# A bank of scores instead of a projection bank for the sample rows' products of every natural block

## The chip, the cores and the metric

The kernel runs on one core of a Trainium2 chip, in one launch. The metric is the device time of the program in microseconds (us), the median of several runs.

## The reference

One inference step of a decoder layer, in f32. There are 1024 prompt rows and 8 sample rows (one new token each for 8 sequences), a model width of 1024 and one combined input projection:

```python
def _project(x, norm_g, w_in, qn_g, kn_g):
    h = _rms(x, norm_g)
    proj = jnp.einsum('bld,dn->bln', h, w_in)
    aq, ak, av, az, bu, bv, bz, cq, cf, ci, cz = jnp.split(proj, cuts, axis=-1)
...
        o_a = _dilated_prompt(aq, ak, av)                        # 12 heads of 64
        o_b, _ = _sgu(bu, bv, sgu_ln_g[l], sgu_ln_b[l], sgu_w[l], sgu_b[l])
        o_c, S_p = _hgrn2(cq, cf, ci, lb_all[l], hgrn_norm_g[l], S0)   # 6 heads of 128
        xp = _merge(xp, o_a, az, o_b, bz, o_c, cz, w_out[l])
```

The same is done for the sample rows, with attention over a cache (`_dilated_step`) and from a given recurrent state. `_merge` multiplies each branch by its gate, projects with `w_out` and adds `x`.

## The kernel before, in words

The stages stand in the program in this order: RMSNorm of the prompt and transposes to `h` (nine tiles `xt0` to `xt8`, each transposed in two `tr0` tiles; `xt8` is the sample rows, kept in f32 as `hs`), then attention, HGRN, SGU, output projection. Attention takes pairs of heads `p` = 0 to 5: block `qk{p}` is projected (four groups `pqk{p}_{g}`), the two heads `p_0` and `p_1` follow (scores for the maximum `s2_...`, transposed scores `st_...`, sums `pv{p}_{h}_{qc}`), and `normalise` (`pb{p}_0`) ends the pair. Blocks `v0` to `v2` (`pv{sp}_{g}`) and `az0` to `az2` serve two pairs each. HGRN has six heads (`c_head`, line 663, with `pn{h}_{half}` its last matmul of a half) fed by blocks `cqf{h}` (`pc...`), `ci0` to `ci2` (`pi...`) and `cz0` to `cz2`; a decode for the sample rows (`pmx`, `pda`, `pdt`) stands between the heads. SGU begins with the blocks `bv0`, `bv1` (`pbv...`), then `bz0` (`pbz0...`), `bu0` and so on.

A *block* is 256 columns of `w_in`, loaded by `load_w` (lines 190 to 208) as four pairs of 128 rows. SyncE (SP) issues the load of each pair into a tile `wr_...` of f32 ("raw"; 6 buffers, so one and a half blocks), ScalarE (ACT) rounds it into `wh_...`, GpSimd (POOL) makes the rest `wl_...` (4 buffers each). A projection is three matmuls for each 128 rows of depth, `h` and `w` each split into a high and a low part. The raw tile is held until its last reader is through: the rounding, the rest, and in the blocks `qk`, `v`, `ci`, `bv` ("natural" blocks: rows on the partitions) also the products of the 8 sample rows, `pss_...`, which take the raw f32 weights: eight matmuls, 16 records in the profile. `add_groups` (line 267) then adds their four groups, with one copy on ACT and three additions on VectorE (DVE), and frees the bank.

PSUM has eight banks: two for projections (`p_proj`), four for scores and all else of that kind (`p_st` and `p_big` share the same four, also the HGRN tiles `pk`, `lv`, `ls`, `pn`), one for transposes and decode (`p_tr`), one for sums (`p_pv`). Before, `pss_...` took a bank of `p_proj`, with the exception of `v0`, whose products and groups take banks of scores.

The order of the instructions on each engine is not the order of the code. The program is handed to a scheduler before the run, which places each instruction by its priority (where it stands in the code) and by when its inputs and a buffer are expected to be free, and hands out the buffers; the order on each engine is then fixed. So a tile that asks for a bank of another kind can move a great part of the program.

Of the kernel before, what the change touches and what calls it, by code (L numbers as in the profile page):

```python
# [91 lines left out]
def hybrid_step(tc, ins, outs, parts=("A", "D", "B", "C", "O"), dbg=None):  # L92
# [9 lines left out]
    with tc.tile_pool(name="const", bufs=1) as cp, tc.tile_pool(name="sb", bufs=1) as sb, \  # L102
# [5 lines left out]
        def inp(nm, shape=(P, L), dt=F32):  # L108
            return sb.tile(list(shape), dt, tag="big", name=nm, bufs=N_BIG)
# [10 lines left out]
        def pq(nm, shape=(P, 512), dt=F32):  # L120
            return sb.tile(list(shape), dt, tag="pq", name=nm, bufs=N_PQ)

        def small(nm, n, p=P, dt=F32, bufs=2, tag=None):
            return sb.tile([p, n], dt, tag=tag or f"sm{n}", name=nm, bufs=bufs)

        def psum(tag, nm, bufs, n=512):
            return pm.tile([P, n], F32, tag=tag, name=nm, bufs=bufs)
# [7 lines left out]
        def p_st(nm):  # L135
            return psum("st", nm, 4)
# [54 lines left out]
        def load_w(cols, nm, spare=False):  # L191
            blk = []
            for i in range(KD // 2):
                if spare:
                    hi = s2(f"wh_{nm}_{i}", F32R, (P, 2, NW))
                    lo = s2(f"wl_{nm}_{i}", F32R, (P, 2, NW)) if i < 2 else ee(f"wl_{nm}_{i}", (P, 2, NW), F32R)
                else:
                    hi = sb.tile([P, 2, NW], F32R, tag="whi", name=f"wh_{nm}_{i}", bufs=N_W)
                    lo = sb.tile([P, 2, NW], F32R, tag="wlo", name=f"wl_{nm}_{i}", bufs=N_WL)
                raw = sb.tile([P, 2, NW], F32, tag="raw", name=f"wr_{nm}_{i}", bufs=N_RAW)  # L200
                o = 0
                for c, w in cols:
                    nc.sync.dma_start(raw[:, :, o:o + w], w_in[:, 2 * i:2 * i + 2, c:c + w])
                    o += w
                nc.scalar.copy(hi, raw)
                nc.gpsimd.tensor_tensor(lo, raw, hi.bitcast(F32), ALU.subtract)
                blk.append((hi, lo, raw))
            return blk
# [10 lines left out]
        for t in (0, NT, *range(1, NT)):  # L219
# [15 lines left out]
            for j in range(2):  # L235
                ps = p_st(f"tr0_{t}_{j}").rearrange("p (a b) -> p a b", a=4)
# [16 lines left out]
        def proj_nat(blk, t, out):  # L253
            for k in range(KD):
                whi, wlo = wsl(blk, k, 0, NW)
                sl = slice(t * P, (t + 1) * P)
                mm(out, h_sl(0, k, sl), whi, k == 0, False)
                mm(out, h_sl(0, k, sl), wlo, False, False)
                mm(out, h_sl(1, k, sl), whi, False, k == KD - 1)

        def rows8(ps, K, i0=0, n=None):

            n = n or len(K)
            for i, (rows, w) in enumerate(K, i0):
                g = 32 * (i % 4)
                mm(ps[g:g + NS, :NW], rows, w, i < 4, i >= n - 4)

        def add_groups(dst, ps):
            nc.scalar.copy(dst, ps[32:32 + NS, :NW])
            for g in (64, 96, 0):  # L270
                nc.vector.tensor_tensor(dst, ps[g:g + NS, :NW], dst, ALU.add)

        def proj_nat_s(blk, nm, bank=None):
            ps = (bank or p_proj)(f"pss_{nm}")
            rows8(ps, [(hs[:, k, :], blk[k // 2][2][:, k % 2, :]) for k in range(KD)])
            dst = small(f"sd_{nm}", NW, NS, tag="sdst")
            add_groups(dst, ps)
            return dst
# [20 lines left out]
        def qk_proj(p, blk=None):  # L299
            blk = blk or load_w([(OFF_Q + p * P, P), (OFF_K + p * P, P)], f"qk{p}")  # L300
            kg = small(f"kg{p}", P, bufs=1, tag="kg")
            nc.sync.dma_start(kg, ins["k_norm_g"][:, p * P:(p + 1) * P].partition_broadcast(P)[:, 0, :])
            st = proj_nat_s(blk, f"qk{p}")
            nats = [inp(f"nat{p}_{i}", (P, 4, NW)) for i in range(2)]
            for g in range(4):
# [34 lines left out]
        def s_out(n):  # L340
            return outs[n][0, :, 0].rearrange("b h e -> b (h e)")
# [3 lines left out]
        def v_proj(sp):  # L345
            blk = load_w([(OFF_V + sp * NW, NW)], f"v{sp}") if sp else blk_v

            bank = p_proj if sp else p_st
            st = proj_nat_s(blk, f"v{sp}", bank)
            V = []  # L350
            for j in range(2):
                vh = inp(f"vh{sp}_{j}", (P, NT, VW), F32R)
                vl = inp(f"vl{sp}_{j}", (P, NT, P), F32R)
                nc.gpsimd.memset(vh.rearrange("p t (h e) -> p t h e", h=2)[:, :, :, E].bitcast(F32), 1.0)
                V.append((vh, vl))
            for g in range(4):
                ps = bank(f"pv{sp}_{g}").rearrange("p (a b) -> p a b", a=2)
                for j in range(2):
                    proj_nat(blk, 2 * g + j, ps[:, j, :])
                vr = pq(f"vr{sp}_{g}", (P, 2, NW))  # L360
                nc.scalar.copy(vr, ps)
                nc.sync.dma_start(new_v[2 * g * P:(2 * g + 2) * P, sp * NW:(sp + 1) * NW]
                                  .rearrange("(a q) c -> q a c", q=P), vr)
                if g < 2:
                    nc.sync.dma_start(v_d[2 * g * P:(2 * g + 2) * P, sp * NW:(sp + 1) * NW]
                                      .rearrange("(a q) c -> q a c", q=P), vr)
                for j in range(2):
                    vh, vl = V[j]
                    t2 = slice(2 * g, 2 * g + 2)
                    hi = vh[:, t2, :].rearrange("p a (h e) -> p a h e", h=2)[:, :, :, 0:E]  # L370
                    src = vr[:, :, j * P:(j + 1) * P].rearrange("p a (h e) -> p a h e", h=2)
                    nc.scalar.copy(hi, src)
                    nc.gpsimd.tensor_tensor(vl[:, t2, :].rearrange("p a (h e) -> p a h e", h=2), src,
                                            hi.bitcast(F32), ALU.subtract)
            nc.sync.dma_start(qkv_d[2, :, sp * NW:(sp + 1) * NW], st)
            nc.sync.dma_start(s_out("o_vs")[:, sp * NW:(sp + 1) * NW], st)
            return V
# [167 lines left out]
        def attention():  # L545
            done = None
            for sp in range(3):
                n0 = qk_proj(2 * sp, blk_first if sp == 0 else None)
                if done:
                    normalise(*done)  # L550
                tiles = qk_layout(2 * sp, n0)
                V = v_proj(sp)
                Z = az_proj(sp)
                done = attn_core(2 * sp, n0, V[0], Z[0], tiles)
                n1 = qk_proj(2 * sp + 1)
                normalise(*done)
                done = attn_core(2 * sp + 1, n1, V[1], Z[1])
            normalise(*done)
# [52 lines left out]
        def c_proj_i(hp):  # L611
            blk = load_w([(OFF_CI + hp * NW, NW)], f"ci{hp}")
            st = proj_nat_s(blk, f"ci{hp}")
            nc.sync.dma_start(qkv_d[3, :, hp * NW:(hp + 1) * NW], st)
            V = [inp(f"V{hp}_{j}", (P, NT, P)) for j in range(2)]
            for g in range(4):
                ps = p_proj(f"pi{hp}_{g}").rearrange("p (a b) -> p a b", a=2)
                for j in range(2):
                    proj_nat(blk, 2 * g + j, ps[:, j, :])
                for j in range(2):  # L620
                    nc.scalar.copy(V[j][:, 2 * g:2 * g + 2, :], ps[:, :, j * P:(j + 1) * P])
            return V
# [475 lines left out]
```

## Time and profile before

| what | value |
|---|---|
| time, median of 3 runs | 1285.43 us (1284.22 to 1287.84) |
| the profiled execution's own time | 1283.54 us |
| its span, first to last instruction | 1281.8 us |
| mean granted TensorE clock | 0.977 |
| TensorE busy (matmuls, PE) | 1206.7 us, 94% |
| VectorE busy (DVE) | 914.1 us, 71% |
| ScalarE busy (ACT) | 669.8 us, 52% |
| GpSimd busy (POOL) | 290.1 us, 23% |

The profiled execution lies 1.9 us under the median, and 1.7 us lie around its span. PE and PEld are the matmuls and the weight loads of TensorE. A granted clock of 1.00 is 2.4 GHz, one of 0.50 is 1.2 GHz. In rows of the trace an "x" is a count, and what stands in square brackets is the time that the engine was idle just before, with what ended it.

### The profile page before, as it was taken

How to read it: one execution, taken by the hardware profiler on the slowest of the kernel's cores; microseconds unless marked ns; L12 is line 12 of the kernel's file. 1: busy time of each engine (PE TensorE's matmuls, PEld its weight loads, DVE VectorE, ACT ScalarE, POOL GpSimd, SP SyncE). 2: the span in 40 equal slices, each digit the busy share in tenths (PEclk: the TensorE clock that was granted, in tenths of full speed). 3: DMA queues.
4: the chain of work that ended last, by engine and by line, in shares of the span. 5: the costliest groups of instructions: out<-in, count | busy, mean ns of one | idle time of the engine just before them, and what ended most of it. 6: DMA issues, size and time to landing. Idle time of an engine off the chain costs nothing.

```text
span 1281.8 us, 27727 instructions
## 1 busy us (share of the span) xinstructions
PE 1206.7 (94%) x10610; PEld 1119.9 (87%) x10610; DVE 914.1 (71%) x2425; ACT 669.8 (52%) x1512; POOL 290.1 (23%) x272
## 2 busy tenths in 40 slices
PE   3899999999999998998999889998999999999998
PEld 2899888998899988987988878887989899899998
DVE  4845888668876786789897898989796534654643
ACT  5445554765547565575445554665443252455543
POOL 4431201312203221122012121111011254122221
PEclk9999999999899998999999889999999999999999
DMA  7241222312223141142253514424253224621110
GB/s 224 68 136 34 65 55 79 108 37 66 71 67 100 42 117 52 25 111 84 67 146 92 131 46 139 127 80 112 81 149 97 84 75 137 194 80 47 62 47 29
DMA packets 165044, 114.17 MB, mean 89 GB/s; under 512 B 13944, under 2 KB 158992, under 8 KB 164912
## 3 DMA queue, kind: packets, MB, share of 16 engines
q1 hardware_dynamic: 157520, 110.28, 29.4%
q10 hardware_dynamic: 6816, 1.54, 0.6%
q8 instruction: 83, 1.36, 0.4%
q0 software_dynamic: 576, 0.58, 0.3%
q14 instruction: 49, 0.40, 0.1%
HBM read 84.47 MB, written 22.09 MB: 83 GB/s over the span
## 4 chain that ended last, share of the span: by engine, by line
PE 72%; DVE 16%; DMA 5%; issue 3%; ACT 3%; SPq 0%; POOL 0%; ACTq 0%; POOLq 0%; DVEq 0%
PE po L100 15%; PE pqk L100 10%; PE pv L100 9%; PE paz L100 5%; PE pi L100 4%; PE pbu L100 4%; PE pbz L100 4%; PE pcz L100 4%; PE pc L100 3%; PE pbv L100 3%; PE st L100 3%; DMA dk<-in_cache_k_dram 2%; PE s L100 2%; DVE T L647 1%; DVE T L649 1%
## 5 line engine op out<-in xcount | busy, mean ns | idle before, releaser
L100 PE MATMUL pqk<-wh_qk,h 128*128 128x256 f32 x768 | 156.6, 294 | 9.1 <-DVE h L243 4.4
L100 PE MATMUL pc<-h,wh_cqf 128*128 128x344 f32 x576 | 144.6, 331 | 10.3 <-DVE cz L152 8.8
L100 PE MATMUL po<-woh,yl 128*128 128x256 f32 x512 | 144.5, 283 | 0.0
L100 PE MATMUL po<-woh,yh 128*128 128x256 f32 x512 | 144.1, 282 | 0.3 <-ACT yh L1046 0.3
L100 PE MATMUL po<-wol,yh 128*128 128x256 f32 x512 | 143.9, 281 | 0.0
L100 PEld LDWEIGHTS pqk<-wh_qk,h 128*128 128x128 f32 x768 | 127.9, 198 | 17.0 <-DVE h L243 5.0
L100 PEld LDWEIGHTS pc<-h,wh_cqf 128*128 128x128 f32 x576 | 102.1, 194 | 13.4 <-DVE cz L152 9.7
L100 PE MATMUL pqk<-wl_qk,h 128*128 128x256 f32 x384 | 112.1, 292 | 0.0
L100 PEld LDWEIGHTS po<-woh,yl 128*128 128x128 f32 x512 | 96.6, 189 | 3.0 <-issue 1.7
L100 PEld LDWEIGHTS po<-woh,yh 128*128 128x128 f32 x512 | 96.3, 188 | 2.1 <-ACT yh L1046 2.1
L100 PEld LDWEIGHTS po<-wol,yh 128*128 128x128 f32 x512 | 96.5, 189 | 0.0
L100 PE MATMUL pc<-h,wl_cqf 128*128 128x344 f32 x288 | 95.3, 333 | 0.0
L455 DVE CUSTOM_DVE_ANT_0 s<-s,masks 128x512 f32<-128x512 f32 (+2 forms) x144 | 77.6, 576 | 19.4 <-PE s L100 18.6
L100 PE MATMUL pi<-wh_ci,h 128*128 128x256 f32 x384 | 79.1, 301 | 10.5 <-DVE cmat L722 8.1
L100 PEld LDWEIGHTS pqk<-wl_qk,h 128*128 128x128 f32 x384 | 75.7, 197 | 1.4 <-issue 0.2
L100 PEld LDWEIGHTS pi<-wh_ci,h 128*128 128x128 f32 x384 | 65.1, 204 | 13.6 <-ACT dsc L962 5.4
L100 PE MATMUL pv<-wh_v,h 128*128 128x256 f32 x384 | 75.2, 287 | 1.0 <-ACT den L516 1.0
L100 PE MATMUL pcz<-h,wh_cz 128*128 128x344 f32 x288 | 71.2, 325 | 0.2 <-DVE q L152 0.2
L100 PE MATMUL paz<-h,wh_az 128*128 128x344 f32 x288 | 68.9, 323 | 0.0
L1047 DVE TENSOR_TENSOR yl<-yb,yh 128x512 fp32r<-128x512 f32 x44 | 30.3, 692 | 52.6 <-ACT yh L1046 52.6
L100 PEld LDWEIGHTS pv<-wh_v,h 128*128 128x128 f32 x384 | 61.1, 189 | 3.1 <-ACT st L493 1.1
L1046 ACT CAST yh<-yb 128x512 fp32r<-128x512 f32 x64 | 39.5, 620 | 42.7 <-PE po L100 41.9
(389 smaller groups left out, 3586.5 us busy)
## 6 DMA issues: line engine op xcount, KB each, us to landing
wro<-in_w_out_dram SPq DMA_DIRECT2D x32, 256.0 KB
wr_qk<-in_w_in_dram SPq DMA_DIRECT2D x48, 128.0 KB
wr_cqf<-in_w_in_dram SPq DMA_DIRECT2D x48, 128.0 KB
dk<-in_cache_k_dram SPq DMA_DIRECT2D x24, 192.0 KB
dv<-in_cache_v_dram SPq DMA_DIRECT2D x24, 192.0 KB
xt<-in_x_prompt_dram SPq DMA_DIRECT2D x8, 512.0 KB
xr<-in_x_prompt_dram SPq DMA_DIRECT2D x32, 128.0 KB
out_o_yp_dram<-xr SPq DMA_DIRECT2D x32, 128.0 KB
```

The lines of the kernel that those rows point to most:

```text
L100: nc.tensor.matmul(out, lhsT=lhsT, rhs=rhs, start=start, stop=stop)
L455: nc.vector.tensor_tensor_reduce(out=ps[:, :w], in0=ps[:, :w], in1=nmask[:, S - n + c:S - n + c + w], op0=ALU.add, op1=ALU.max, scale=1.0, ...
L647: nc.vector.tensor_tensor(K.rearrange("p (n w) -> p n w", w=w), g3[:, :, w - 1:w].to_broadcast([P, 4 * n, w]), h3, ALU.subtract)
L649: nc.vector.tensor_tensor(Q[:, 0:3], g4[:, 1:4], g4[:, 0:3, :, w - 1:w].to_broadcast([P, 3, n, w]), ALU.subtract)
L1046: nc.scalar.copy(yh[:, sl, :], y)
L1047: (nc.gpsimd if piece == 0 else nc.vector).tensor_tensor(yl[:, sl, :], y, yh[:, sl, :].bitcast(F32), ALU.subtract)
```

## The change

`proj_nat_s` takes a bank of scores for every block, and its argument `bank` goes. In `v_proj` the groups `pv{sp}_{g}` keep their own kind of bank.

```diff
-        def proj_nat_s(blk, nm, bank=None):
-            ps = (bank or p_proj)(f"pss_{nm}")
+        def proj_nat_s(blk, nm):
+            ps = p_st(f"pss_{nm}")
             rows8(ps, [(hs[:, k, :], blk[k // 2][2][:, k % 2, :]) for k in range(KD)])
             dst = small(f"sd_{nm}", NW, NS, tag="sdst")
             add_groups(dst, ps)
@@
             bank = p_proj if sp else p_st
-            st = proj_nat_s(blk, f"v{sp}", bank)
+            st = proj_nat_s(blk, f"v{sp}")
```

The same instructions are issued, none more and none less: 13 tiles `pss_...` (`qk0` to `qk5`, `v1`, `v2`, `ci0` to `ci2`, `bv0`, `bv1`) change banks. But each engine's order differs in many places. Three of them:

The first is the start, on SP, which issues the loads: `xt` are the prompt's tiles, `wr_v0` and `wr_az0` weights, `ko` and `K1` results and rows of attention. Before:

```order
L222 DMA xt2_197<-in_x_prompt_dram 128x1024
L222 DMA xt3_224<-in_x_prompt_dram 128x1024
L203 DMA wr_v0_2_373<-in_w_in_dram 128x2x256
L203 DMA wr_v0_3_379<-in_w_in_dram 128x2x256
L222 DMA xt4_251<-in_x_prompt_dram 128x1024
L222 DMA xt5_278<-in_x_prompt_dram 128x1024
L203 DMA wr_az0_0_1015<-in_w_in_dram 128x2x256
L203 DMA wr_az0_1_1021<-in_w_in_dram 128x2x256
L222 DMA xt6_305<-in_x_prompt_dram 128x1024
L222 DMA xt7_332<-in_x_prompt_dram 128x1024
```

With the change:

```order
L222 DMA xt2_197<-in_x_prompt_dram 128x1024
L222 DMA xt3_224<-in_x_prompt_dram 128x1024
L222 DMA xt4_251<-in_x_prompt_dram 128x1024
L222 DMA xt5_278<-in_x_prompt_dram 128x1024
L222 DMA xt6_305<-in_x_prompt_dram 128x1024
L222 DMA xt7_332<-in_x_prompt_dram 128x1024
L320 DMA out_o_kp_dram<-ko0_0_489 128x2x128
L320 DMA out_o_kp_dram<-ko0_1_552 128x2x128
L203 DMA wr_v0_2_373<-in_w_in_dram 128x2x256
L203 DMA wr_v0_3_379<-in_w_in_dram 128x2x256
```

All prompt tiles are now issued one behind the other, and the second half of block `v0` after them. On DVE the scaling of `qkg` (line 323), the first rows of `lb` (lines 570 to 575) and the additions of `sd_qk0` (line 271), which stood between the first prompt tiles, stand behind the last one.

The second is head 1_1 of attention on PE, between its scores `s2_1_1_...`. The rows `pv1_1` are projections of block `v1`. Before:

```order
L100 MATMUL s2_1_1_6_0_2186<-KK1_1_1910,QQ1_1_1912 128x512
L100 MATMUL pv1_1_2818<-wh_v1_1_2723,h10_82 128x256
L100 MATMUL s2_1_1_6_512_2189<-KK1_1_1910,QQ1_1_1912 128x384
L100 MATMUL pv1_1_2818<-wh_v1_2_2729,h01_81 128x256
L100 MATMUL pv1_1_2818<-wl_v1_2_2730,h01_81 128x256
L100 MATMUL pv1_1_2818<-wh_v1_2_2729,h11_83 128x256
L100 MATMUL pv1_1_2818<-wh_v1_2_2729,h01_81 128x256
L100 MATMUL pv1_1_2818<-wl_v1_2_2730,h01_81 128x256
L100 MATMUL pv1_1_2818<-wh_v1_2_2729,h11_83 128x256
L100 MATMUL pv1_1_2818<-wh_v1_3_2735,h01_81 128x256
L100 MATMUL pv1_1_2818<-wl_v1_3_2736,h01_81 128x256
L100 MATMUL s2_1_1_7_0_2192<-KK1_1_1910,QQ1_1_1912 128x512
```

With the change:

```order
L100 MATMUL pv1_1_2818<-wh_v1_1_2723,h10_82 128x256
L462 MATMUL pm1_1_0_2168<-ident_65,M1_1_0_2155 4x128
L100 MATMUL s2_1_1_5_512_2183<-KK1_1_1910,QQ1_1_1912 128x256
L100 MATMUL s2_1_1_6_0_2186<-KK1_1_1910,QQ1_1_1912 128x512
L100 MATMUL s2_1_1_6_512_2189<-KK1_1_1910,QQ1_1_1912 128x384
L100 MATMUL s2_1_1_7_0_2192<-KK1_1_1910,QQ1_1_1912 128x512
L100 MATMUL s2_1_1_7_512_2195<-KK1_1_1910,QQ1_1_1912 128x512
L100 MATMUL st1_1_0_0_2205<-QQ1_1_1912,KK1_1_1910 128x512
L100 MATMUL st1_1_0_0_2205<-Q11_1_1913,K11_1_1911 128x512
```

No projection stands between the scores any more: of `v1` only the pairs 0 and 1 are used up to here, in two unfinished groups, and `pss_qk2`, which still reads the raw tiles of block `qk2`, comes behind the last score tile of this head (`st1_1_1_3`) and the transposes `tr2_1`. Before, it stood in head 0_1, behind `st0_1_0_0`. Counted from the last score tile of head 1_0 (`st1_0_1_3`) to `pb1_0` there were 180 projection matmuls of 256 columns, and there are 55; from `st3_0_1_3` to `pb3_0`, the same place for head 3_1, there were 171, and there are 15. The same stretch has 120 instead of 158 in head 0_1, 158 instead of 155 in head 2_1, and 158 instead of 180 in head 4_1.

The third is the end of HGRN on PE: `pc5_0_2` is the last projection of head 5, `pmb4` decode 4, `pn5_1` the last matmul of head 5, `pda5` and `pdt5` decode 5. Before:

```order
L100 MATMUL pc5_0_2_11627<-h11_83,wh_cqf5_3_11465 128x344
L100 MATMUL pc5_0_2_11627<-h01_81,wl_cqf5_3_11466 128x344
L100 MATMUL pss_bv0_12273<-wr_bv0_0_12251,hs_79 8x256 x2
L100 MATMUL pss_bv0_12273<-wr_bv0_1_12257,hs_79 8x256 x2
L100 MATMUL pss_bv0_12273<-wr_bv0_2_12263,hs_79 8x256 x2
L100 MATMUL pss_bv0_12273<-wr_bv0_3_12269,hs_79 8x256 x2
L960 MATMUL pmb4_11388<-ident_65,dmb4_11385 128x16
L100 MATMUL pbv0_0_12288<-wh_bv0_0_12249,h00_80 128x256
```

With the change:

```order
L100 MATMUL pn5_1_12065<-csq5_1_12062,ones_67 128x512
L100 MATMUL pda5_12152<-dv5_1_0_12172,dsc5_12103 32x128
L100 MATMUL pda5_12152<-dv5_1_1_12178,dsc5_12103 32x128 x4
L100 MATMUL pss_bv0_12273<-wr_bv0_0_12251,hs_79 8x256 x2
L100 MATMUL pss_bv0_12273<-wr_bv0_1_12257,hs_79 8x256 x2
L100 MATMUL pss_bv0_12273<-wr_bv0_2_12263,hs_79 8x256 x2
L100 MATMUL pss_bv0_12273<-wr_bv0_3_12269,hs_79 8x256 x2
L100 MATMUL pda5_12152<-dv5_1_2_12185,dsc5_12103 32x128 x4
L100 MATMUL pss_bv1_12520<-wr_bv1_0_12498,hs_79 8x256 x2
L100 MATMUL pss_bv1_12520<-wr_bv1_1_12504,hs_79 8x256 x2
L100 MATMUL pss_bv1_12520<-wr_bv1_2_12510,hs_79 8x256 x2
L759 MATMUL pdt5_12193<-ident_65,pdt5s_12191 128x128 x2
```

`pss_bv0` has moved from ahead of block `bv0` to the very end of head 5 and decode 5. From `pn4_0` to `pn5_1` there stood 264 matmuls of 256 columns of `bv0` and `bv1` and 113 of 344 columns of `bz0`; with the change 120 of `bv0` and `bv1` (96 that end `bv0`, and 24 that use the pairs 0 and 1 of `bv1`). Of the rest of `bv1`, 168 matmuls stand behind `pda5`, ahead of `bz0`, where 11 stood before.

## Rows read from the trace of the kernel before

**Rows 1.** The page: busy time by engine, and the chain that ended last.
```profile
PE 1206.7 (94%) x10610; PEld 1119.9 (87%) x10610; DVE 914.1 (71%) x2425; ACT 669.8 (52%) x1512; POOL 290.1 (23%) x272
...
PE 72%; DVE 16%; DMA 5%; issue 3%; ACT 3%; SPq 0%; POOL 0%; ACTq 0%; POOLq 0%; DVEq 0%
```

**Rows 2.** Windows of one tile: us, PE, PEld, DVE (ACT) busy, clock, DMA share, GB/s.
```profile
75.64:87.91 12.27, 11.88 (x96) 11.31 (x95) 0.00 (x0) 1.17 (x2) 1.00 0.42 114
91.53:106.67 15.14, 15.14 (x98) 15.14 (x97) 2.07 (x4) 1.00 0.00 1
```

**Rows 3.** DVE and SP, timeline of the start: start, us, line, operation, idle before.
```profile
30.00 0.17 DVE L323 TENSOR_SCALAR qkg<-qkg 128x6 f32<-128x6 f32 x1 [6.28 <-DMA qkg<-in_q_norm_g_dram]
36.23 0.17 DVE L570 TENSOR_TENSOR lb<-lb 128x6 f32<-128x6 f32 x1 [1.62 <-DMA lb<-in_hgrn_lb_logits_dram]
58.38 0.68 DVE L243 TENSOR_TENSOR h<-tr,h 128x512 fp32r<-128x512 f32 x1
...
20.07 0.90 SPq L203 DMA_DIRECT2D wr_v<-in_w_in_dram  x2
21.02 0.93 SPq L222 DMA_DIRECT2D xt<-in_x_prompt_dram  x2
27.69 7.25 SPq L222 DMA_DIRECT2D xt<-in_x_prompt_dram  x2
```

**Rows 4.** Window of the start: us, PE, PEld, DVE, ACT, POOL busy, clock.
```profile
18.00:60.00 42.00, 33.92 (x257) 29.77 (x258) 31.88 (x82) 20.91 (x54) 17.21 (x12) 0.96 0.38 99
```

**Rows 5.** Windows of heads 1_1 and 3_1, columns as in rows 4.
```profile
201.60:234.30 32.70, 32.70 (x268) 31.50 (x267) 24.66 (x61) 16.03 (x34) 0.43 (x1) 1.00 0.19 57
353.40:387.00 33.60, 32.61 (x264) 31.07 (x263) 26.48 (x67) 16.49 (x34) 0.73 (x1) 1.00 0.22 66
```

**Rows 6.** DVE, groups by line, 201.6 to 234.3: count, busy, mean, idle before.
```profile
L455 DVE CUSTOM_DVE_ANT_0 s<-s,masks 128x512 f32<-128x512 f32 (+3 forms) x12 | 6.5, 573 | 2.9 <-PE s L100 2.8
L508 DVE TENSOR_TENSOR pl<-st,ph 128x512 fp32r<-128x512 f32 (+2 forms) x9 | 5.6, 636 | 0.4 <-PE pv L100 0.3
...
L428 DVE SCALAR_TENSOR_TENSOR KK<-tr,qkg,KK 64x512 fp32r<-64x512 f32 x3 | 2.2, 748 | 3.1 <-ACT KK L425 3.1
```

**Rows 7.** POOL, timeline: the rest of block v0's last two pairs.
```profile
23.61 2.51 POOL L206 TENSOR_TENSOR wl_v<-wr_v,wh_v 128x512 fp32r<-128x512 f32 x2 [7.11 <-DMA wr_v<-in_w_in_dram]
```

**Rows 8.** PE, timeline: idle time at sample rows' products and at groups behind them.
```profile
310.60 0.36 PE L100 MATMUL pqk<-wh_qk,h 128*128 128x256 f32 x1 [1.29 <-DVE sd_qk L271]
603.20 1.05 PE L100 MATMUL pss_ci<-wr_ci,hs 128*8 128x256 f32 x16 [0.48 <-DVE q L152]
607.35 0.55 PE L100 MATMUL pi<-wh_ci,h 128*128 128x256 f32 x1 [3.10 <-DVE cmat L722]
754.46 0.55 PE L100 MATMUL pi<-wh_ci,h 128*128 128x256 f32 x1 [4.97 <-DVE cmat L722]
892.57 1.88 PE L100 MATMUL pss_bv<-wr_bv,hs 128*8 128x256 f32 x16 [3.33 <-DVE q L152]
```

**Rows 9.** Windows of HGRN and of its end, columns as in rows 4.
```profile
565.70:919.40 353.70, 324.02 (x3492) 295.63 (x3491) 305.46 (x866) 190.31 (x452) 63.35 (x54) 0.96 0.38 105
...
917.30:997.00 79.70, 77.63 (x974) 71.38 (x973) 65.53 (x237) 35.85 (x95) 10.31 (x8) 0.98 0.38 108
919.40:998.30 78.90, 76.83 (x909) 71.10 (x908) 65.78 (x241) 35.48 (x93) 10.31 (x8) 0.98 0.37 106
```

**Rows 10.** DVE, groups by line, 919.4 to 998.3.
```profile
L850 DVE BATCH_NORM_STATS2 st<-vraw 128x6 f32<-128x256 f32 x16 | 5.7, 411 | 0.2 <-PE pda L100 0.2
L858 DVE TENSOR_SCALAR vraw<-vraw,mv 128x512 f32<-128x512 f32 x8 | 3.9, 542 | 0.0
L749 DVE TENSOR_TENSOR cz<-cz,pn 128x512 f32<-128x512 f32 x4 | 2.7, 676 | 4.9 <-ACT pn L748 4.9
```

**Rows 11.** Windows of tile pi behind an idle time of PE: clock behind PE, PEld, ACT.
```profile
607.30:613.50 6.20, 6.15 (x31) 6.18 (x32) 0.00 (x0) 0.56 0.36 104
613.50:619.70 6.20, 5.78 (x47) 5.44 (x46) 0.65 (x2) 1.00 0.01 1
```

## Prediction

> **What bounds the kernel now.** The page comes first: TensorE's matmuls fill 94% of the span, and the chain that ended last lies on PE for 72% and on DVE for 16% [rows 1]. So PE is the bound, and only in the mean: attention heads, HGRN heads and the decode are chains that run through ACT, DVE and PE in turn, and PE is full there because projection matmuls of a later block stand between the steps of the chain. I call these matmuls the filler. What the change is worth is read from stretches, by how much filler lies beside which chain.
>
> The windows show it. From the last score tile of head 1_0 to the end of head 1_1, 201.6 to 234.3, PE is busy 32.70 of 32.70 us, and DVE 24.66 [rows 5]. The change's section counts 180 projection matmuls in this stretch. A stretch of nothing but such matmuls has 96 in 12.27 us, 0.128 us each [rows 2], so the filler is 23.0 us and PE's own part of the head 9.7. The same stretch of head 3_1 has 171 in 33.60 us: 21.9 filler, 11.7 the rest. In HGRN, DVE is busy 305.46 of 353.70 us, and PE 324.02 [rows 9]: two engines near their limit. At the end of HGRN it is 77.63 on PE and 65.53 on DVE of 79.70 [rows 9]. There is also idle time on PE right at the tiles that change banks: 0.48 and 3.10 us at `ci1`, 4.97 at `ci2`, 3.33 at `bv0`, and 1.29 where a group of `qk4` waits for the addition that frees its bank [rows 8], 13.2 in all. It is what a freed projection bank could give back.
>
> **What the change does.** Nothing is computed more or less. A tile `pss` now asks for one of the four banks of scores, for which the score tiles and HGRN tiles that stand earlier in the program ask too, and these go first. The order shows the outcome: `pss_qk2` stands behind the last score tile of head 1_1, `pss_bv0` behind nearly all of head 5 and decode 5. Until `pss` has run, its block's four raw tiles stay held. Six exist, so the next block gets two pairs, and its projections stop after half of each group: with two projection banks these are 2 x 12 matmuls. That is why the order has 24 matmuls of `v1` in head 1_1 and 24 of `bv1` in head 5, and then none. I take this as a property of the order, which is fixed; what the holes cost is the question.
>
> *The start.* On DVE the scaling of `qkg` waited 6.28 us and the first row of `lb` 1.62 us, each for a small load, in the middle of the prompt tiles [rows 3]. These rows, and the additions of `sd_qk0`, now stand behind the last tile. SP's loads of `xt4` to `xt7` no longer stand behind weights (the issues at 21.02 and 27.69). The last tile was through on DVE at 58.38 + 0.68. From 18 to 60 PE was busy 33.92 of 42.00 us [rows 4], so 8.1 us of idle time is what can be won, with a little beside it for the clock. The tiles have a chain of their own and will not let PE have it all: I take -6, bounds -9 and -3.
>
> *Heads 1_1 and 3_1.* With 55 and 15 filler matmuls instead of 180 and 171, PE has 7.0 + 9.7 = 16.7 us of work in the one and 1.9 + 11.7 = 13.6 in the other, and the head's own chain sets the length. DVE's work in the stretch is 24.66 us; some 2 of these are the sample rows' steps and not the head's, and the chain has waits of its own, as the 2.9 before the score maxima and the 3.1 before the layout's row [rows 6], of which I count 3. That makes 26 us, and 26 for head 3_1 too, whose DVE time is 26.48 with as much beside it. The 125 and 156 matmuls that were beside the head come later, at 0.128 us: 16.0 and 20.0. So 26 + 16.0 - 32.7 = +9.3 and 26 + 20.0 - 33.6 = +12.4, together **+21.7**. Bounds: a chain of 23 us (DVE without a wait) gives +15.7; one of 30 gives +29.7.
>
> *The other heads.* Head 0_1 has 38 matmuls less beside it (4.9 us), head 4_1 22 less (2.8 us), and head 2_1 about as many. By the same sum PE is left with about the length of the chain, so little is lost, but the filler that is left comes with half its weights late: two pairs took 6.0 us from their issue at 20.07 to the end of their rest at 26.12 [rows 3, 7]. The 1.29 us at `qk4` goes the other way. Together +3, bounds 0 and +8.
>
> *HGRN up to head 4.* The waits at `ci1`, `ci2` and `bv0` sum to 11.9 us [rows 8]. They are waits of matmuls that stood ahead of a chain's, so a free bank alone doesn't end them: PE was late for DVE there, which is busy 86% of the time [rows 9]. I credit half, -6, and take 2 off it for the pairs that load late: -4, bounds -12 and +4.
>
> *The end of HGRN.* From `pn4_0` to `pn5_1` there were 264 x 0.128 = 33.8 us and 113 matmuls of 344 columns at 15.14 / 96 = 0.158 us [rows 2], 17.9 us: 51.7 of filler in 79.70 us. Now there are 120, 15.4 us, so PE has 26 + 15.4 = 41 us of work there, and the chain sets the length. DVE's 65.53 us have some 18 of the next stage in them, the statistics and scaling of `bv` (5.7 and 3.9 us) [rows 10] and small rows, which follow their matmuls out. 47.5 us stay; the waits of the chain itself, like the 4.9 before line 749, I put at 10: 58 us instead of 79.7. What comes behind is 144 x 0.128 + 113 x 0.158 = 36.3 us of PE, with nothing beside it, and ahead of it the second half of `bv1`, whose raw tiles only `pss_bv0` frees: 6.0 us as above, of which the rest of decode 5 hides one. 58 + 36.3 + 5 - 79.7 = **+19.6**. Bounds: 50 us and no wait for the load, +7; 66 us and all of it, +29. The DVE rows that come later lie beside matmuls.
>
> *The clock.* Behind the idle time of 3.10 us at 607.35 the granted clock was 0.56 for 6.2 us, in which 31 matmuls ran; in the next 6.2 us, at 1.00, it was 47 [rows 11]. 31 matmuls are 4.0 us at 0.128, so one such hole cost 2.2 us more than its idle time. Three new stretches where PE is thin: +4, bounds 0 and +7.
>
> **The sum.** -6 + 21.7 + 3 - 4 + 19.6 + 4 = +38.3, on the profiled execution's own 1283.54 us: **1322 us**. That execution is 0.15% under the median of 1285.43, which is inside what a measurement of this kernel can tell from no change, about 0.3%; I don't correct for it. The terms' bounds, taken as independent, give some 15 us to either side.
>
> **The rivals.**
> *The change gains* (faster). The holes are no holes on the chip: ACT and DVE run their chains ahead as PE's filler no longer stands in their way, and the stretches shrink by as much as comes back later. Then what is left are the gains: up to 9 at the start and 13.2 of idle time, 1283.5 - 22 = 1261 us. It decides where holes and late loads cost less than these 22 us; my sum has 44 for them (48 with the clock). For it speaks that every one of the waits in rows 8 is at the resource that the change relieves. Against it: DVE alone has 24.66 and 26.48 us of work in the bare heads [rows 5], so chains under 23 us can't be, and at that bound the two heads and the end still cost 15.7 + 7. The Trainium skill ("Perfetto Trace Analysis", section Optimization Strategy under Identifying Performance Opportunities) says that a gap that repeats on the engine that should be saturated can mean too little SBUF or PSUM for the next tile, which would speak for this rival, as two banks for all projections are the scarce kind here; by that rule alone the sum would be the gains. The trace has the gaps, but they are not steady ones, and the order moves the scarcity to the raw tiles.
> *A small loss.* The chains take their lower bounds: heads +15.7, end +10, no clock, start -6, HGRN -6, others 0: +14, 1297 us. It differs from the forecast by size alone; it decides if DVE's waits inside a bare head are near nothing.
> *A larger loss.* Two raw tiles are too few elsewhere too. Each of the eight natural blocks from `qk2` to `bv0` releases its raw tiles late, and if PE then runs dry for a part of the 6.0 us each time, 2.5 in the mean, that is 20 us more: 1342, and with a lower clock behind each 1350.
> *The change does nothing.* Only if the order made no difference. With 55 for 180 matmuls in a stretch it can only come by gains equal to losses.
>
> **How the numbers follow.** The forecast, with 1305 to 1345 as its own range, has 0.60. The small loss, 1288 to 1305, has 0.16, the larger one, over 1345, 0.12, the gain 0.08, and no change 0.04. Faster is 0.08, same 0.04, slower 0.88. Under 1294 lie the gain, no change and a small part of the small loss, about 0.15, over 1350 some 0.06, so the range is 1294 to 1350.
>
> **What would show it.** In the profile after: the waits at lines 323 and 570 are gone from the prompt tiles, and the last line 243 is 5 to 10 us earlier; in heads 1_1 and 3_1 PE is busy for half the time or less, with `pss_qk2` and `pss_qk4` at their ends and loads of `wr` right behind them; from `pn4_0` to `pn5_1` it is some 58 us, followed by a block `bv1` of 20 us and more without another engine near its limit; the clock is under 1 where PE fills up again. PE's busy time is about the same, and its idle time some 35 us more. I am wrong if the bare heads are under 20 us, if `bv1`'s late half costs nothing and the end of HGRN shrinks by more than 35 us, or if the late pairs hold PE up at many blocks.

## The result, and the profile after

The changed kernel takes 1332.69 us (median of 4 runs, 1331.20 to 1339.27) against 1284.83 us (4 runs) before: a ratio of 1.0392, 95% interval 1.0364 to 1.0420, some 50 us slower by the ratio and 48 between the medians. The forecast was 1322 us with 1294 to 1350. The profiled execution took 1333.2 us, its span is 1331.4 us and its mean granted clock 0.965.

The page of the changed kernel, busy time by engine:

```profile
PE 1232.4 (93%) x10610; PEld 1130.5 (85%) x10610; DVE 904.8 (68%) x2425; ACT 676.5 (51%) x1512; POOL 301.9 (23%) x272
```

Beside [rows 1] PE has the same 10610 instructions, 25.7 us more of busy time, and 24 us more of idle time. So half of the loss doesn't look like waiting at all; that comes back below.

The stages, cut at the same instructions in both kernels: from the end of block `az0`, where the first scores start, to the end of block `cz0`, from there to `pn4_0`, from there to `pn5_1`, from there to the end of `bz0`, and the rest. Columns are us, then busy us of PE, PEld, DVE, ACT and POOL with their counts, the granted clock, the DMA share and GB/s. After:

```profile
107.93:573.68 465.75, 450.05 (x3292) 410.90 (x3291) 336.18 (x857) 265.12 (x546) 94.97 (x101) 0.97 0.23 64
573.68:929.62 355.94, 316.30 (x3309) 289.96 (x3309) 292.06 (x843) 187.23 (x438) 68.43 (x51) 0.95 0.34 98
929.62:993.31 63.69, 47.20 (x723) 38.58 (x723) 53.77 (x191) 24.30 (x60) 3.33 (x4) 0.84 0.44 120
993.31:1048.95 55.64, 54.02 (x429) 48.52 (x428) 30.52 (x90) 20.67 (x50) 9.62 (x8) 1.00 0.33 100
1048.95:1331.40 282.45, 277.77 (x2217) 259.64 (x2216) 131.04 (x301) 120.93 (x290) 82.41 (x59) 1.00 0.26 80
```

The same cuts in the kernel before:

```profile
110.61:568.43 457.82, 441.54 (x3299) 407.86 (x3301) 345.88 (x867) 264.42 (x548) 94.74 (x101) 0.98 0.24 67
568.43:916.78 348.35, 318.67 (x3399) 291.25 (x3399) 301.19 (x858) 186.03 (x444) 61.23 (x53) 0.96 0.38 105
916.78:995.83 79.05, 76.98 (x971) 71.02 (x970) 64.86 (x236) 35.70 (x94) 10.31 (x8) 0.98 0.39 111
995.83:1003.37 7.54, 7.54 (x45) 5.77 (x45) 7.44 (x13) 4.29 (x10) 3.40 (x3) 1.00 0.30 101
1003.37:1281.80 278.43, 274.68 (x2261) 261.62 (x2260) 137.05 (x310) 120.50 (x291) 77.96 (x58) 1.00 0.27 84
```

The end of `az0` comes 2.7 us earlier (107.93 for 110.61). Attention takes 7.9 us more, HGRN up to `pn4_0` 7.6 more (with 3.1 us of projections fewer ahead of that mark, so 10.7), its end with what stands behind it 119.33 for 86.59, 32.7 more (29.7 by the same count), the rest 4.0 more. With the 2.7 us at the start taken off, the sum is 49.6, which is the whole difference of the spans.

The two heads that the order left bare, from the last score tile of the head before (`st1_0_1_3`, `st3_0_1_3`) to `pb1_0` and `pb3_0`; first the change, then the kernel before with the same two marks (the windows of [rows 5] ended 1.5 and 0.6 us short of them):

```profile
190.66:217.33 26.67, 24.63 (x181) 19.50 (x180) 24.30 (x60) 15.92 (x34) 3.28 (x3) 0.94 0.17 44
351.71:377.25 25.54, 22.63 (x142) 17.52 (x140) 22.59 (x54) 13.59 (x27) 0.73 (x1) 0.80 0.14 36
```
```profile
201.62:235.79 34.17, 34.17 (x279) 32.74 (x277) 25.79 (x62) 17.31 (x36) 0.97 (x2) 1.00 0.20 58
353.35:387.60 34.25, 33.26 (x269) 31.62 (x268) 26.85 (x67) 16.78 (x35) 0.73 (x1) 1.00 0.23 67
```

DVE has 24.30 and 22.59 us of work in 26.67 and 25.54: the head's own chain sets the length. With the 125 and 156 projections that come later, 26.67 + 16.0 - 34.17 = +8.5 and 25.54 + 20.0 - 34.25 = +11.3. PE is called busy for 92% and 89% of these stretches, with 181 and 142 records where there were 279 and 269.

The projections come back behind the heads. From `pb1_0` to `st2_0_1_3` the order has 358 instead of 230, from `pb3_0` to `st4_0_1_3` 358 instead of 221; first the change, then the kernel before:

```profile
217.33:277.95 60.62, 60.62 (x447) 57.53 (x446) 31.83 (x80) 35.77 (x73) 19.54 (x22) 1.00 0.33 96
377.25:438.16 60.91, 60.78 (x447) 57.47 (x446) 31.84 (x80) 35.83 (x73) 19.54 (x22) 1.00 0.33 98
```
```profile
235.79:282.67 46.88, 46.00 (x331) 43.08 (x330) 28.70 (x74) 31.68 (x67) 16.37 (x20) 1.00 0.28 82
387.60:433.46 45.86, 45.23 (x323) 42.05 (x322) 28.98 (x73) 32.60 (x67) 16.81 (x20) 1.00 0.29 86
```

That is 13.7 + 15.1 = 28.8 us more for 265 matmuls, which at 0.128 us would be 33.9.

What the late products hold up stands in the queue's own timeline. SP issues the second half of block `v1` at 214.29, while `pss_qk2` ran from 213.64 to 214.69, and the second half of `bv1` at 995.29, with `pss_bv0` from 994.61 to 995.86; POOL had been idle for 42.42 us ahead of it:

```profile
214.29 0.89 SPq L203 DMA_DIRECT2D wr_v<-in_w_in_dram  x2
...
995.29 0.89 SPq L203 DMA_DIRECT2D wr_bv<-in_w_in_dram  x2
...
998.96 2.51 POOL L206 TENSOR_TENSOR wl_bv<-wr_bv,wh_bv 128x512 fp32r<-128x512 f32 x2 [42.42 <-ACT wh_bv L205]
```

### The profile page after: what moved, and what is told of

Its sections match the earlier page's. It is cut to its first block, busy times and chain, and to the rows that moved or that the text cites. A ratio compares the mean times of both kernels' runs of the same rounds, so it can differ in the third digit from the quotient of the medians.

```text
span 1331.4 us, 27739 instructions
## 1 busy us (share of the span) xinstructions
PE 1232.4 (93%) x10610; PEld 1130.5 (85%) x10610; DVE 904.8 (68%) x2425; ACT 676.5 (51%) x1512; POOL 301.9 (23%) x272
## 5 line engine op out<-in xcount | busy, mean ns | idle before, releaser
L100 PE MATMUL pc<-h,wh_cqf 128*128 128x344 f32 x576 | 145.8, 335 | 12.5 <-DVE cz L152 7.3
L100 PE MATMUL pv<-wh_v,h 128*128 128x256 f32 x384 | 72.4, 285 | 0.9 <-DVE nat L315 0.9
L100 PE MATMUL pi<-wl_ci,h 128*128 128x256 f32 x192 | 58.8, 307 | 4.7 <-POOL wl_ci L206 4.7
```

The costliest lines, as they stand in the source:

```text
L100: nc.tensor.matmul(out, lhsT=lhsT, rhs=rhs, start=start, stop=stop)
```

## The experiments

All times are medians of their runs; the kernel before was timed on the same chip in each set (1284.65, 1283.05 and 1285.16 us), and ratios are to it. A difference in us given right behind a ratio is worked out from the ratio; between the medians it can be up to 3 us less (25.1 for e1's 27.9). The first five put some of the products back into a projection bank (`p_proj`); nothing else is edited.

**e1: the end of HGRN alone.**
```diff
-            ps = p_st(f"pss_{nm}")
+            ps = (p_st if nm[:2] in ("v0", "bv") else p_proj)(f"pss_{nm}")
```


> Only the products of bv0 and bv1 take a bank of scores; qk, v, ci keep a projection bank. Theory (late products hold raw tiles, the next block comes with half its weights, and the chain is left bare): the order is that of the kernel before up to the end of HGRN and that of the change from there, so the loss of that place alone, +25 to +34 us over before, about 1314. Rival (a tile of products takes a score bank from the scores, a little at each of 13 places): 2 of 13 parts of the loss of 48, +7, 1292.

1309.74 us, ratio 1.0217 (1.0182 to 1.0252): +27.9 us.

**e2: everything but the end of HGRN.**
```diff
-            ps = p_st(f"pss_{nm}")
+            ps = (p_proj if nm[:2] == "bv" else p_st)(f"pss_{nm}")
```


> The change, but bv0 and bv1 in a projection bank again. Theory: the end of HGRN is as before, the rest of the loss stays: 1333 - 30 = 1303. Rival (a little at each of 13 places): 1326.

1299.43 us, ratio 1.0129 (1.0090 to 1.0169): +16.6 us. The two together give 44.5 of the change's 50, so two of 13 products carry about half of the loss or more, and at one place. The stretches `pn4_0` to `pn5_1` and from there to the end of `bz0` in the profile of e1:

```profile
914.78:976.38 61.60, 47.03 (x690) 37.23 (x689) 50.97 (x188) 22.89 (x60) 3.25 (x4) 0.83 0.38 106
976.38:1030.51 54.13, 52.00 (x392) 47.44 (x394) 25.78 (x73) 19.51 (x46) 9.60 (x8) 0.97 0.30 90
```

and in that of e2:

```profile
921.52:1000.22 78.70, 77.95 (x1016) 68.90 (x1017) 58.20 (x206) 34.31 (x81) 10.48 (x10) 1.00 0.46 131
1000.22:1017.88 17.66, 17.66 (x114) 17.12 (x113) 16.71 (x60) 9.18 (x25) 2.20 (x2) 1.00 0.35 116
```

e1 has 61.60 + 54.13 us there, close to the change's 63.69 + 55.64. e2 has 78.70 + 17.66 for the 79.05 + 7.54 of before; 72 projections that stood ahead of `pn4_0` before stand behind it in e2, and at 0.128 us these are 9.2 of the 9.8 us. The loss by a share for each product is out.

**e3: the start alone.**
```diff
-            ps = p_st(f"pss_{nm}")
+            ps = (p_st if nm in ("v0", "qk0") else p_proj)(f"pss_{nm}")
```


> Only the products of qk0 take a bank of scores (v0 has one already). Theory: the start of the change alone, 2.7 us less at the first head's scores, and the order of before from there: -3 us, about 1282. Rival (the start's gain is given back where its loads stand): 1285, and heads 0_0 and 0_1 not earlier.

1278.12 us (10 runs), ratio 0.9958 (0.9941 to 0.9976): -5.4 us. It is the one version that beats both kernels clear of its interval. The gain in the profile is 1.3 us at the first score and 4.3 in attention, so most of it comes later than I had it, and why it comes there no run shows. This product too is late and holds its raw tiles: `pss_qk0` runs at 54.10 instead of from 18.95, and the second half of block `v0` is issued right behind it, at 54.75 instead of the 20.07 of [rows 3]:

```profile
54.10 1.05 PE L100 MATMUL pss_qk<-wr_qk,hs 128*8 128x256 f32 x16
...
54.75 0.89 SPq L203 DMA_DIRECT2D wr_v<-in_w_in_dram  x2
```

**e4: attention alone.**
```diff
-            ps = p_st(f"pss_{nm}")
+            ps = (p_st if nm[0] in "qv" else p_proj)(f"pss_{nm}")
```


> The products of qk0 to qk5, v1 and v2 in banks of scores, those of ci and bv in a projection bank. Theory: the bare heads 1_1 and 3_1 (+8.5 and +11.3 in the profile of the change), the start and other gains, as there: +5 at the start of HGRN, and no more behind it, 1290. Rival (the loss in HGRN comes from what attention leaves late, not from ci): +15 at head 4 of HGRN, 1300.

1280.84 us (10 runs, 1274.36 to 1290.40), ratio 0.9980 (0.9953 to 1.0006): no change that can be told. Its profile lost 10.7 us in attention and won 12.5 in HGRN up to `pn4_0`, whose products have their old banks; the order there differs in small things only, and what won them stays open.

**e5: HGRN's `ci` alone.**
```diff
-            ps = p_st(f"pss_{nm}")
+            ps = (p_st if nm == "v0" or nm[:2] == "ci" else p_proj)(f"pss_{nm}")
```


> Only the products of ci0 to ci2 take a bank of scores. Theory (late products, half blocks): HGRN loses as in the change, +11 to +16 us from its start to head 4, 1285 + 13 = 1298. Rival (the prediction's own term: the waits at ci are relieved): -4, 1281.

1297.27 us, ratio 1.0114 (1.0090 to 1.0138): +14.6 us. The prediction's own term for HGRN, -4, has the wrong sign. The place is wider than expected, though: in the profile 4.9 us stand up to `pn4_0` (6.8 with 15 projections fewer ahead of that mark), 6.4 from there to the end of `bz0` and 4.7 behind it.

**e6 to e8: is it the bank, or where the products stand?** In e6 the products get a bank of their own, and the scores have three:
```diff
-            return psum("st", nm, 4)
+            return psum("st", nm, 3)
...
+        def p_own(nm):
+            return psum("own", nm, 1)
...
-            ps = p_st(f"pss_{nm}")
+            ps = (p_own)(f"pss_{nm}")
```


> All 13 products and v0's in one bank of their own, and the scores have three banks instead of four. In the order the products then stand early and no head is bare. Theory (what costs is that products wait behind scores and hold raw tiles): no loss at the heads and at the end, 1275 to 1290, not over the control with three score banks. Rival (score banks are what is scarce): the change's loss stays or grows, 1320 and more.

e7 has three score banks and the products where they were before:
```diff
-            return psum("st", nm, 4)
+            return psum("st", nm, 3)
...
+            ps = (p_st if nm == "v0" else p_proj)(f"pss_{nm}")
```


> The kernel before with three score banks instead of four, the eighth bank empty: the control for the bank of its own. Theory: the heads are bound by PE with filler, so three banks cost little: 1285 to 1295. Rival (score banks are what is scarce): 1310 and more.

e8 leaves the scores their four banks and puts the products into the bank of transposes:
```diff
-            ps = p_st(f"pss_{nm}")
+            ps = (p_st if nm == "v0" else p_tr)(f"pss_{nm}")
```


> All products but v0's in the one bank of transposes and decode, the scores' four banks untouched. In the order heads 1_1 and 3_1 and the end of HGRN are bare again (16, 15 and 39 us of projections less beside them), since the products wait behind transposes and decode there. Theory: about the change's time, 1320 to 1340. Rival (the scores lose by the bank that products take from them): about before, 1285 to 1295.

e6: 1287.98 us, ratio 1.0040 (1.0025 to 1.0054). e7: 1310.89 us, 1.0214 (1.0176 to 1.0252). e8: 1327.49 us, 1.0349 (1.0306 to 1.0393). Products that come early cost nothing: e6 is 23 us under its control. Products that come late cost 44.8 us, nearly as much as in the change, though they take no bank from the scores: e8, whose profile has the thin stretches again, here heads 1_1 and 3_1 between the marks used above and `pn4_0` to `pn5_1`. (What it costs by itself that they share the one bank of the transposes, no run separates.)

```profile
202.18:227.30 25.12, 22.40 (x147) 16.46 (x146) 21.97 (x55) 14.11 (x32) 2.63 (x4) 0.86 0.17 52
361.09:385.31 24.22, 21.41 (x147) 15.34 (x146) 21.41 (x54) 13.85 (x31) 2.65 (x4) 0.93 0.18 53
929.63:990.57 60.94, 46.48 (x716) 36.71 (x715) 52.14 (x190) 23.02 (x60) 2.80 (x4) 0.89 0.38 108
```

The rival is right in one point that I had put low: a fourth score bank is worth 27 us (e7), and e6 pays for it. In the profiles both pay in attention, 480.6 and 483.0 us for 457.8. Behind it, from the end of `cz0` to the end of `bz0`, the kernel before, e7 and e6 have:

```profile
568.43:1003.37 434.94, 403.18 (x4411) 368.04 (x4412) 373.48 (x1105) 226.02 (x547) 74.94 (x64) 0.96 0.38 106
```
```profile
595.28:1028.23 432.95, 404.84 (x4395) 369.93 (x4392) 371.09 (x1101) 225.32 (x546) 82.69 (x66) 0.96 0.36 101
```
```profile
592.31:1003.33 411.02, 395.47 (x4390) 357.45 (x4391) 372.53 (x1098) 220.26 (x538) 82.91 (x66) 1.00 0.40 112
```

So where the products leave the projection banks and wait behind nothing, HGRN and its end are 24 us shorter than before and 22 shorter than in the control, at a clock of 1.00 instead of 0.96. That is as much as the prediction's rival of a gain counted on; in the change the products wait, and there is none of it.

**e9 to e12: the raw tiles.** Two more of them need the room of one of the 16 large tiles (the first number), so e9 is the change with that one gone, and e10 has the two raw tiles as well (the last number but one):
```diff
-N_BIG, N_S2, N_S2B, N_PQ, N_W, N_WL, N_GT, N_RAW, N_E = 16, 6, 2, 5, 4, 4, 2, 6, 3
+N_BIG, N_S2, N_S2B, N_PQ, N_W, N_WL, N_GT, N_RAW, N_E = 15, 6, 2, 5, 4, 4, 2, 6, 3
```


> The change, with 15 instead of 16 of the large tiles (what two more raw tiles need in room): the control for the next run. At heads 1_1 and 3_1 and at the end of HGRN the order has as many projections as the change. Theory: about the change's loss, +48, 1325 to 1340. Rival (large tiles are scarce): 1345 and more.

```diff
-N_BIG, N_S2, N_S2B, N_PQ, N_W, N_WL, N_GT, N_RAW, N_E = 16, 6, 2, 5, 4, 4, 2, 6, 3
+N_BIG, N_S2, N_S2B, N_PQ, N_W, N_WL, N_GT, N_RAW, N_E = 15, 6, 2, 5, 4, 4, 2, 8, 3
```


> The change with 15 large tiles and eight raw weight tiles instead of six, so that a block whose products are late leaves room for a whole next block. The products stand as late as in the change or later. Theory (held raw tiles cut the next block in half): heads 1_1 and 3_1 have their projections again (0.8 more and 0.3 less than before in us, where the change has 20.0 and 18.8 less), the end of HGRN half (17.9 less instead of 39.4), and the weight waits in HGRN go: 35 to 45 us under the control, 1285 to 1300. Rival (late products cost by themselves, or by the score banks): within 10 us of the control, 1320 and more.

e9: 1339.43 us, ratio 1.0425 (1.0404 to 1.0447). e10: 1310.95 us, 1.0196 (1.0172 to 1.0221), 28.5 us under e9. Windows of heads 1_1 and 3_1, of `pn4_0` to `pn5_1` and of what follows up to the end of `bz0`, in e9:

```profile
198.18:222.86 24.68, 20.94 (x158) 15.85 (x157) 23.85 (x60) 14.91 (x32) 0.74 (x1) 1.00 0.16 43
...
359.65:383.63 23.98, 21.26 (x157) 15.90 (x157) 23.19 (x58) 14.50 (x31) 0.73 (x1) 1.00 0.16 44
935.74:1001.51 65.77, 44.83 (x733) 36.88 (x731) 50.37 (x187) 23.79 (x60) 3.05 (x4) 0.82 0.39 112
1001.51:1055.62 54.11, 51.99 (x394) 47.27 (x394) 26.23 (x75) 19.52 (x46) 9.62 (x8) 0.97 0.30 90
```

and in e10:

```profile
203.16:241.00 37.84, 37.84 (x314) 34.70 (x313) 25.79 (x57) 16.68 (x33) 0.74 (x1) 1.00 0.21 62
...
355.45:390.53 35.08, 35.08 (x292) 31.91 (x291) 24.76 (x57) 15.65 (x31) 0.74 (x1) 1.00 0.23 67
921.67:990.89 69.22, 62.61 (x908) 56.14 (x908) 54.20 (x193) 27.94 (x67) 6.32 (x6) 0.98 0.40 112
990.89:1026.44 35.55, 33.10 (x218) 26.84 (x220) 26.75 (x80) 15.03 (x42) 7.14 (x6) 0.95 0.44 141
```

The heads have 314 and 292 records beside a DVE chain of about the same length, and PE is full; the end takes 104.8 us instead of 119.9. From the end of `cz0` to `pn4_0` e10 takes 347.8 us for e9's 355.5, and PE waits 4.5 us for weights there instead of 7.6. In e10 `pss_qk2` comes no earlier than in e9, at the end of head 1_1 (237.26 to 241.07, up to `pb1_0`), so late products alone leave no head bare: the raw tiles that they hold do. It is 28.5 us and not the 35 to 45 expected. The control for the raw tiles without late products is the kernel before with the same line as e10:

> The kernel before with 15 large tiles and eight raw tiles: does more room for weights help where the products are early? Theory: nothing at the heads; the end of HGRN has 14 us of projections less beside it in the order, so +3 to +10, 1288 to 1295. Rival (raw tiles were short before too): 1275 and less.

1295.85 us, ratio 1.0098 (1.0061 to 1.0135): more raw tiles and one large tile less cost 11 to 13 us there (medians and ratio); the profile has 8.3 more at the end of HGRN (`pn4_0` to the end of `bz0`) and 4.3 behind it. So of e10's 25 to 26 us over before, 11 to 13 are that exchange, and if the two simply add up, 13 to 15 still belong to late products. At last the exchange with only attention's products in score banks:
```diff
+N_BIG, N_S2, N_S2B, N_PQ, N_W, N_WL, N_GT, N_RAW, N_E = 15, 6, 2, 5, 4, 4, 2, 8, 3
...
+            ps = (p_st if nm[0] in "qv" else p_proj)(f"pss_{nm}")
```


> Products of qk and v in banks of scores, of ci and bv in a projection bank, 15 large tiles and eight raw tiles. Theory: what the change gains in attention (about 12 us beside the bare heads' 20) without the bare heads, and the cost of the run before at the end of HGRN: 1268 to 1278, under the kernel before. Rival (the gain in attention came from the thin filler itself): 1285 and more.

1309.65 us (5 runs), ratio 1.0193 (1.0170 to 1.0217): a miss by over 30 us. In the profile the first score came 3.0 us later than before instead of earlier, attention took 15.5 us more with both heads covered, and HGRN had none of e4's 12.5. What the change wins elsewhere in attention doesn't stay when the bare heads are mended. How much is lost instead isn't sharp: attention takes 4.6 us more in e10, with the same heads covered, and 5.0 more in e11, where no product is late.

## Why the prediction was right, and where its terms were off

The mechanism held where the forecast had most of the loss, in the bare heads and at the end of HGRN: 19.8 + 29.7 us measured for 21.7 + 19.6. The total came 10.7 us over the forecast. Two terms were off by far more than their bounds, the other heads by -14.9 us and HGRN up to head 4 by +14.7; that they cancel is luck: had the other heads cost the 3 us that I took, the time would have been some 1347 us, close to the end of the range at 1350. The start and the end of HGRN lie 0.3 and 0.7 us outside theirs.

**The start**, -6: measured -2.7. The waits at lines 323 and 570 left the prompt tiles, as said, and the last line 243 ended at 54.23 instead of 59.06, 4.8 us earlier. But the wait for `qkg` is still there behind them, 3.31 us, and PE was busy 34.90 of 42.00 us from 18 to 60, for 33.92 in [rows 4], at a lower clock:

```profile
18.00:60.00 42.00, 34.90 (x283) 31.98 (x281) 34.11 (x79) 20.66 (x54) 16.79 (x10) 0.92 0.26 86
```
```profile
59.71 0.42 DVE L323 TENSOR_SCALAR qkg<-qkg 128x6 f32<-128x6 f32 x1 [3.31 <-DMA qkg<-in_q_norm_g_dram]
```

**Heads 1_1 and 3_1**, +21.7: measured 8.5 + 11.3 = +19.8. The chain of 26 us was 26.67 and 25.54. The sum takes the projections that come later at 0.128 us each; behind the heads they came 5.1 us cheaper, as shown above, and these are counted in the next term.

**The other heads**, +3 with 0 to +8: measured 7.9 - 19.8 = -11.9, outside its bounds. I had counted only the projections that these heads lose, and taken the heads before as free of waits because PE was called busy. Of the 11.9 us, 5.1 come back right behind the bare heads, and only 1.4 of these are idle time of PE that went; the rest is spread over the other stretches by at most 2.6 us each. What gives it back is not settled. In e10 and e12, which cover the bare heads again, the gain is gone. The profiles of one order also differ by some 6 us over attention (the change +7.9, e2 +2.1), so the size is not sharp either. e4's time can't stand for this: its total of about zero is 10.7 us lost in attention against 12.5 won in HGRN.

**HGRN up to head 4**, -4 with -12 to +4: measured +10.7. The step that failed is the 2 us for pairs that load late. PE's groups by line in HGRN of the changed kernel, 573 to 945, with the idle time ahead of them and its releasers, and `cz`'s of the kernel before, the only such wait there:

```profile
L100 PE MATMUL pc<-h,wh_cqf 128*128 128x344 f32 x480 | 121.8, 337 | 12.5 <-DVE cz L152 7.3 <-ACT wh_cqf L205 2.8 <-DVE q L152 2.4
L100 PE MATMUL pc<-h,wl_cqf 128*128 128x344 f32 x240 | 81.3, 343 | 1.5 <-POOL wl_cqf L206 1.5
L100 PE MATMUL pcz<-h,wh_cz 128*128 128x344 f32 x195 | 47.5, 325 | 1.1 <-ACT wh_cz L205 1.1
L100 PE MATMUL pi<-wl_ci,h 128*128 128x256 f32 x128 | 39.6, 310 | 3.8 <-POOL wl_ci L206 3.8
L100 PE MATMUL pcz<-h,wl_cz 128*128 128x344 f32 x98 | 32.1, 331 | 3.2 <-POOL wl_cz L206 3.2
L100 PE MATMUL pbv<-wl_bv,h 128*128 128x256 f32 x58 | 17.0, 293 | 1.9 <-POOL wl_bv L206 1.9
```
```profile
L100 PE MATMUL pcz<-h,wl_cz 128*128 128x344 f32 x97 | 31.9, 330 | 0.7 <-POOL wl_cz L206 0.7
```

Waits for weights are 2.8 + 1.5 + 1.1 + 3.8 + 3.2 + 1.9 = 14.3 us in 15 waits, instead of 0.7: the mechanism of the larger loss, whose rival had 20 us for all blocks, those of attention too, where the same waits are 2.3 us (it counted eight blocks from `qk2` to `bv0`; there are ten). It is also one of the signs that I had named for being wrong, late pairs that hold PE up at many blocks. PE's idle time in this stage is 10.0 us more, which is nearly all of the loss.

The credit of 6 us for the waits in [rows 8] is less clear. By the view of waits PE waited 27.2 us for DVE in this stage before, and 20.9 with the change, 6.3 less. But a freed bank isn't shown to have done it: e5, with `ci` alone moved, has 29.7 (and 5.6 for weights), and e4, whose `ci` stays in a projection bank, has 16.7. And a wait can pass to another instruction: the 4.97 us at `ci2` are gone, and 4.16 us for the next line of DVE that fills a `cmat` stand ahead of `pmx2`, which the order puts there now. Rows of the view of waits: who waits in which line, for which engine and line, us, times, the longest; the second row is that of 929.62 to 993.31:

```profile
PE pmx L955 <- DVE cmat L723: 4.2, 1, 4.2
```
```profile
PE pd L100 <- DVE ysT L978: 5.9, 1, 5.9
```

**The end of HGRN**, +19.6 with +7 to +29: +29.7 in the profile of the change, +27.9 by the times of e1. The stretch is 63.69 us and not 58, with 5.9 us in one wait of `pd5`, the sample rows' step of head 5, for DVE, the second of these rows; what follows takes 48.1 us more instead of 41.3, with tiles of SGU in it that stood behind `bz0` before. The late half of `bv1` came as said.

**The clock**, +4. The granted clock was 0.80 in head 3_1 and 0.84 at the end, where it was 0.62 while PE was busy 2.00 of 8.00 us, and 0.50, 1.2 GHz, in the next 8 us with 4.02 busy:

```profile
962.00:970.00 8.00, 2.00 (x18) 0.72 (x18) 8.00 (x37) 2.44 (x8) 0.00 (x0) 0.62 0.31 84
970.00:978.00 8.00, 4.02 (x14) 3.21 (x14) 5.92 (x18) 0.11 (x1) 0.00 (x0) 0.50 0.59 145
```

Time below the full clock is (1 - 0.965) x 1331.4 = 46.6 us for (1 - 0.977) x 1281.8 = 29.5. What these 17 us cost can't be read off, since DVE's chain runs beside them. In the two heads it is little: e2 has the same 55 and 15 projections beside them at clocks of 1.00 and 0.93 instead of 0.94 and 0.80, and takes 26.07 and 24.01 us, 0.6 and 1.5 less. For the end no run tells it.

**The rest**, taken as 0, is 4.0 us longer; e1 and e5 have it too (4.3 and 4.7), e2 to e4 less (2.4, 0.5 and 0.0). Its cause stays open.

**The rivals.** The gain was wrong for this change: the order moved the scarcity from the projection banks to the raw tiles (e8 and e10). What the gain counted on exists where the products wait behind nothing: e6 is 23 us under its control, and its HGRN and end are 24 us under the kernel before. The Trainium skill's rule on repeated gaps ("Perfetto Trace Analysis", Optimization Strategy), against which the prediction had set the order, is that they can mean too little SBUF or PSUM for the next tile. By that rule e6 is what one expects, and the changed kernel is not. e3 has 5.4 of the gain's 22 us, with a late product of its own.

Two of the signs didn't come. PE's busy time was to be about the same and its idle time some 35 us more; they are 25.7 and 24 us more. And PE's half-busy heads can't be seen in its busy share: the records get fewer and longer.

## What to carry to other kernels

A tile moved to another kind of buffer takes the place in the queue of those it now competes with: look what it reads and holds while it waits, since that (here two thirds of the weight tiles) is what runs short, not the buffer that was freed. Count filler beside each dependent chain in the instruction order: what is taken from a chain comes back behind it, here at 28.8 us for the 33.9 that these matmuls take alone. Sum the waits of a stage before and after; one wait that went can stand at another instruction. A bank in which the moved tile waits behind nothing (e6) kept what was to be gained, though here it cost the scores a bank. The one move that gained over all (e3) held weight tiles too, but there the loads that it held had stood between those of the prompt.

## What was not expected of the hardware

PE's busy share hides a thin stretch. The records of matmuls overlap: the 480 of the first group of HGRN shown above have a mean of 337 ns, 161.8 us together, and cover 121.8 us. In a stretch with fewer of them a record covers more: 24.63 us for 181 records in head 1_1, 34.17 for 279 before, so 136 ns a record instead of 122, and in head 3_1, at a clock of 0.80, 159 instead of 124. How much of this is less overlap, how much the clock and how much that other kinds of matmul are left, no run separates. With 25.7 us more of busy time for the same 10610 instructions the share of PE doesn't show the hole. The count of records does, and so do the weight loads (PEld): they are busy 19.50 of 26.67 us and 17.52 of 25.54 in the two heads, 73% and 69%, where they had 96% and 92%.
